# Output projection and the first MLP's first two sets: TensorE's instructions in the order in which they are written

## The chip, the cores and the metric

The kernel runs on one core of a Trainium2 chip. The metric is the device time of one execution in microseconds, the median of the runs. The core has five engines with a queue each: TensorE (PE in the profile, with its weight loads as PEld), VectorE (DVE), ScalarE (ACT), GpSimd (POOL) and SyncE (SP, which here issues most DMAs). Each engine runs its queue in order; an instruction that waits for another engine holds up what stands behind it in its own queue.

## The reference

The model is a two-layer decoder trunk on x of 1024 tokens by 1024 channels, in float32. Layer 0 mixes tokens by a gated linear recurrence with 8 heads, layer 1 by a causal convolution; a squared-ReLU MLP with 4096 hidden units follows each, and every block ends in a DeepNorm layer norm. The change lies where layer 0's mixer ends and its MLP begins:

```python
mix = o.astype(h.dtype) @ w_out                  # o: normalised, gated output of the recurrence
x = layer_norm(DEEPNORM_ALPHA * x + mix, ln_mix_g[0], ln_mix_b[0])
ff = jnp.square(jax.nn.relu(x @ ffn_w1[0])) @ ffn_w2[0]
```

## The kernel before

**Precision and tiles.** Every float32 operand of a large product is split into a high part, rounded to the matrix unit's format, and a low part, the rest. `product` sums high*high, high*low and low*high in one PSUM bank: three matmuls of 128x128 by 128x512 for each 128 of depth. Tokens are split into two halves of 512, a half into four blocks of 128 (t = 0 to 3).

**Seven products in place of eight.** The MLP's products follow Strassen's scheme in the Winograd form: from four quarters of a weight block and four of x come seven forms, taken in the order `ORDER = (1, 2, 6, 5, 7, 3, 4)`. Forms 1 and 2 of x (`xf[1]`, `xf[2]`) come from the first half of the tokens alone, forms 5 and 6 from both halves, forms 7, 3 and 4 last (`x1_late`).

**Output projection** (the loop `for half in range(2)`). A product for token block t and output half n is 8 parts of three matmuls, 24 in all. Three products of the first half, blocks 0, 1, 2 with n = 0, are done earlier, within the tail of the recurrence. The loop then takes for the first half (t, n) = (0,1), (1,1), (3,0), (2,1), (3,1), and for the second all eight in order. DVE adds each result to the residual y. With a block's n = 1 the block is complete, and `x1_block` normalises it: two halves of statistics, their aggregate, an add, a power on POOL, and two scaled passes over the block, all on DVE but the power. It also stores the block (`keep`) and puts jobs on a list, `bg.chores`.

**The list of jobs.** `product` takes one job off the list when its matmuls are written (`bg.chore()`), so a job's instructions stand behind the product that took it. A job of the first half (`turn`) transposes half a block on TensorE (four transposes of 128x128, operands `ident` and `y`) into one of two banks, and ACT and DVE split the result into `xf`. The loop calls `bg.chore()` once more behind `x1_block` of blocks 1, 2 and 3 of the first half. A job of the second half is `x1_first` (four transposes of the left half of the channels, then DVE makes and splits form 5) or `x1_second` (the right half; forms 6, 4 and parts of 3 and 7). For the second half's last block, t = 3, the two are put on the list behind the loop, among empty jobs that only count products.

**The first MLP** (`Up`). Its first matrix is worked through in eight sets c of seven forms; a form is two products (q = 0, 1) of 4 parts, 12 matmuls. Sets 0 and 1 begin out of turn with forms 1 and 2, the early products, from weights split in advance (`early`); then the loop goes on with the forms left, c = 0 and c = 1, and with sets 2 to 7. `fw` loads the four quarters of a set's weights, sums and splits them into forms on DVE and ACT; a buffer of its raw quarters comes free when the last norm of the second half no longer needs its gain and bias.

**Order.** Up to the end of the recurrence all five engines run in the order written (`tc.manual_schedule` with the five engines, closed by `order.close()`). From there on the framework's scheduler chooses each engine's order by its own timing model, and may move an instruction past others that are written earlier, also into the hand-ordered stretch ahead. The names of the profile: `ps` are the eight PSUM banks, `w` and `oT` the projection's operands, `x1f` and `fw` the MLP's, `c` the copies of MLP products, `xf` and `fs` the operands of the layer's input products, whose last ones run in the tail of the recurrence, and `o` the recurrence's output before its own transposes (`ident,o`). Line 204 is the helper through which TensorE and DVE work is recorded.

Of the kernel before, what the change touches and what calls it, by code (L numbers as in the profile page):

```python
# [21 lines left out]
NTB = HT // P  # L22
# [246 lines left out]
def body(ctx, tc, d, out):  # L269
# [10 lines left out]
    def view(kb, shape, dt=F32, name="t"):  # L280
        at, top = int(kb * 1024), KBYTES * 1024
        if at < edge[0]:
            if edge[0] < top:
                space.tile([P, (top - edge[0]) // 4], F32, name="gap")
            edge[0] = 0
        if at > edge[0]:
            space.tile([P, (at - edge[0]) // 4], F32, name="gap")
        edge[0] = at + (prod(shape) + 7) // 8 * 32
        return space.tile([P, *shape], dt, name=name)
# [33 lines left out]
    bg = Background()  # L323
# [47 lines left out]
    order = ExitStack()  # L371
# [12 lines left out]
    def later(n, job):  # L384
        if n:
            waiting.append((ticks[0] + n, job))
        else:
            job()
# [10 lines left out]
    def block_sums(name, layer, c, after=None, gap=0, adds=None):  # L399

        t = sums[name, layer, c] = dram.tile([4, P, 1024], F32, name=f"sum_{name}{layer}{c}")
        v, w = t.rearrange("a p n -> p a n"), d[name][layer, c].rearrange("a p n -> p a n")
        queue = nc.sync if after is not None else nc.gpsimd
        if adds is not None:

            def copies(rows, after):
                nc.sync.dma_start(out=t[0:4:2, rows.start, 0:1], in_=after)
                queue.dma_start(out=v[rows, 0:2], in_=w[rows, 0:4:2])
                queue.dma_start(out=v[rows, 2:4], in_=w[rows, 0:2])

            copies(slice(16, P), after)
            adds.append(lambda after: copies(slice(0, 16), after))
            adds.append(lambda after: nc.gpsimd.dma_start(out=v[:, 0:2], in_=w[:, 2:4], accum_op=ALU.add))
            for i in (2, 3):
                adds.append(lambda after, i=i: nc.gpsimd.dma_start(out=v[:, i], in_=v[:, i - 1], accum_op=ALU.add, max_dma_last_dim=4096))
            return
        if after is not None:
            nc.sync.dma_start(out=t[0:4:2, 0, 0:1], in_=after)
        queue.dma_start(out=v[:, 0:2], in_=w[:, 0:4:2])
        later(gap // 2, lambda: queue.dma_start(out=v[:, 2:4], in_=w[:, 0:2]))  # L420
        parts = [lambda: nc.gpsimd.dma_start(out=v[:, 0:2], in_=w[:, 2:4], accum_op=ALU.add)]
        for i in (2, 3):
            parts.append(lambda i=i: nc.gpsimd.dma_start(out=v[:, i], in_=v[:, i - 1], accum_op=ALU.add, max_dma_last_dim=4096))
        for i, part in enumerate(parts):
            later((i + 1) * gap, part)
# [75 lines left out]
    for k in range(4):  # L501
        c = slice((k % 2) * HT, (k % 2 + 1) * HT)
# [533 lines left out]
    tick(100)  # L1036
    assert not waiting and not loaded and not to_load and not gates, (waiting, gates)
    order.close()
    oT = [o[0] for o in oT]


# [108 lines left out]
    def of(x, t, i=slice(None)):  # L1150
        return x[..., t * P : (t + 1) * P] if i == slice(None) else x[:, i, :, t * P : (t + 1) * P]

    def turned(yt, k0):
        pt = aux()
        for j in range(4):
            tensor.transpose(pt[:, j, :], yt[:, (k0 + j) * P : (k0 + j + 1) * P], ident)
        return pt

    def less(out, x, y):
        vector.tensor_tensor(out=out, in0=x, in1=y, op=ALU.subtract)  # L1160

    def minus_both(out, x, y):
        vector.scalar_tensor_tensor(out=out, in0=x, scalar=-1.0, in1=y, op0=ALU.mult, op1=ALU.subtract)

    def spot(t, k):
        if t < NTB - 1:
            return of(late_x[(7, 3)[k]], NTB - 1)
        return y[1][:, NTB - 2, k * HT : (k + 1) * HT].rearrange("p (a b) -> p a b", a=4)

    def x1_split(i, t, src):  # L1170
        split(of(xf[i], t, 0), of(xf[i], t, 1), src)

    def x1_first(t):
        s, pt = spot(t, 0), turned(y[1][:, t, :], 0)
        less(s, of(xf[1], t, 0).bitcast(F32), pt)
        vector.tensor_tensor(out=s, in0=s, in1=of(xf[1], t, 1).bitcast(F32), op=ALU.add)
        x1_split(5, t, s)
        temp[t], x01[t] = s, pt

    def x1_second(t):  # L1180
        s, pt = spot(t, 1), turned(y[1][:, t, :], 4)
        minus_both(s, temp[t], pt)
        nc.scalar.copy(out=of(late_x[3], t), in_=pt)
        less(of(late_x[7], t), of(late_x[3], t), x01[t])
        x1_split(6, t, s)
        x4 = of(late_x[4], t)
        minus_both(x4, s, of(xf[2], t, 0).bitcast(F32))
        less(x4, x4, of(xf[2], t, 1).bitcast(F32))

    def x1_late(i, k):  # L1190
        nc.gpsimd.tensor_copy(out=xf[i][:, 0, k, :1], in_=fw.queue[0][:, 1, :1].bitcast(F32))
        split(xf[i][:, 0, k : k + 2], xf[i][:, 1, k : k + 2], late_x[i][:, k : k + 2])
# [262 lines left out]
    fw.todo = [[(blocks("w1q", 0, c), 2 if c < 2 else 0)] for c in range(NFC)]  # L1455
    up = Up()

    bg.chores += [lambda: None, lambda: x1_first(NTB - 1), lambda: x1_second(NTB - 1)] + [lambda: None] * 3
    bg.chores += [lambda i=i, k=k: x1_late(i, k) for i in (7, 3, 4) for k in (0, 2)]
    up.form(0, 1, early[0].take(1)[0])  # L1460
    up.form(0, 2, early[1].take(1)[0], late=True)
# [6 lines left out]
    for c in range(NFC):  # L1468
        for i in ORDER[2 if c < 2 else 0 :]:
            (f,) = fw.take(1)  # L1470
            fw.ahead(3)
            if (c, i) == (0, 7):
                bg.done()
            up.form(c, i, f)
        if c in (0, 2):
            block_sums(*to_sum.pop(0), f[:2, 1, :1].bitcast(F32))
        if c == 0:
            up.settle(1)
            hold += [view(208, (2, 1024), F32, "spare"), view(216, (1024,), F32, "next")]
# [478 lines left out]
```

## Time and profile before

| | |
|---|---|
| time, median of 3 runs | 2057.86 us (2054.11 to 2058.38) |
| the profiled execution | 2059.69 us, its span 2057.9 us |
| granted TensorE clock, mean | 0.998 |
| PE busy | 2026.5 us, 98% |
| DVE busy | 1487.4 us, 72% |
| ACT busy | 1092.0 us, 53% |
| POOL busy | 392.1 us, 19% |
| projection's matmuls (w, oT) | x384, 415.7 to 512.5 us |
| first MLP's first product (x1f, fw) | x1344, 513.1 to 827.6 us |

A row of a timeline gives start, length, engine, line, operation, output and inputs, size and count, and in brackets the idle time of the engine ahead of it with the instruction that ended it. Rows of one kind in sequence are merged.

### The profile page before, as it was taken

Reading aid. Unit: us, or ns where it says so; the run is one execution under the profiler, and the core shown is the slowest. Engines: PE = TensorE matmul, PEld = TensorE weight load, DVE = VectorE, ACT = ScalarE, POOL = GpSimd, SP = SyncE. Lnnn points to the kernel's source line nnn. Section 1 sums busy time; section 2 is a strip of 40 time slices with the busy share of each in tenths; the row PEclk is TensorE's granted clock in tenths of the full one; section 3 lists DMA queues with packets and bytes.
Section 4 is the critical chain, followed back from the end, with each engine's and each line's share of the span. In section 5 each row is a group of like instructions: output and inputs, shape, how many; then the busy total and the mean of one; then the engine's idle time right before and its main releaser. Section 6 shows DMA issues by size and latency. Waiting matters only on the chain. (4 is left out here: it accounts for less than half of the span.)

```text
span 2057.9 us, 29631 instructions
## 1 busy us (share of the span) xinstructions
PE 2026.5 (98%) x11144; PEld 1670.6 (81%) x11144; DVE 1487.4 (72%) x1978; ACT 1092.0 (53%) x1725; POOL 392.1 (19%) x393
## 2 busy tenths in 40 slices
PE   8999999999999999999999999999999999999998
PEld 7888887788787888888888888888888887888886
DVE  8698887877966665666567898889589666754456
ACT  5456565631654555444443776488625555443343
POOL 0112222111100000000001699079110000100002
PEclk9999999999999999999999999999999999999999
DMA  4788989842689786999998854587759778995542
GB/s 187 221 200 228 261 240 252 268 187 82 180 295 307 243 286 224 372 338 325 338 336 301 308 185 184 194 330 272 255 215 343 241 231 297 392 294 197 194 154 102
DMA packets 183944, 517.55 MB, mean 251 GB/s; under 512 B 17912, under 2 KB 49784, under 8 KB 182776
## 3 DMA queue, kind: packets, MB, share of 16 engines
q1 hardware_dynamic: 168312, 456.93, 61.8%
q0 software_dynamic: 15488, 58.72, 12.3%
q8 instruction: 87, 1.43, 0.3%
q14 instruction: 57, 0.47, 0.1%
HBM read 380.85 MB, written 201.85 MB: 283 GB/s over the span
## 5 line engine op out<-in xcount | busy, mean ns | idle before, releaser
L204 PE MATMUL ps<-dw,dh 128*128 128x512 f32 x2688 | 611.1, 389 | 0.0
L204 PEld LDWEIGHTS ps<-dw,dh 128*128 128x128 f32 x2688 | 504.2, 188 | 104.6 <-DVE dh L204 0.2
L204 PE MATMUL ps<-x1f,fw 128*128 128x512 f32 x1344 | 309.7, 392 | 4.6 <-ACT c L1266 2.5
L204 PEld LDWEIGHTS ps<-x1f,fw 128*128 128x128 f32 x1344 | 252.5, 189 | 60.3 <-ACT c L1266 3.6
L204 PE MATMUL ps<-xf,fs 128*128 128x512 f32 x1008 | 250.0, 399 | 3.7 <-issue 2.0
L204 POOL TENSOR_TENSOR cb<-cb,prod 128x512 f32<-128x512 f32 x168 | 223.1, 1337 | 12.5 <-ACT prod L1589 2.0
L204 DVE TENSOR_TENSOR dh<-dh 128x1024 fp32r<-128x1024 f32 x112 | 136.5, 1222 | 116.1 <-ACT dh L72 112.7
L204 PEld LDWEIGHTS ps<-xf,fs 128*128 128x128 f32 x1008 | 185.1, 189 | 43.3 <-issue 2.2
L204 DVE SCALAR_TENSOR_TENSOR ps<-u,par,ps 128x512 f32<-128x512 f32 x296 | 206.1, 749 | 11.0 <-ACT ps L1601 9.5
L204 PE MATMUL ps<-xa,wa 128*128 128x512 f32 x864 | 203.0, 392 | 0.1
L72 ACT CAST dh<-dh 128x1024 fp32r<-128x1024 f32 x112 | 117.4, 1051 | 156.0 <-DMA dh<-hf 148.9
L204 PEld LDWEIGHTS ps<-xa,wa 128*128 128x128 f32 x864 | 160.3, 188 | 33.2 <-ACT ha L1331 0.3
L72 ACT CAST dw<-dr 128x1024 fp32r<-128x1024 f32 x112 | 117.3, 1052 | 131.0 <-PE ps L204 115.3
L204 DVE TENSOR_TENSOR dw<-dr,dw 128x1024 fp32r<-128x1024 f32 x112 | 136.3, 1222 | 69.5 <-ACT dw L72 68.4
L1589 ACT ACTIVATE prod<-u,par 128x512 f32<-128x512 f32 x168 | 119.8, 726 | 37.1 <-POOL cb L204 36.7
L518 POOL TENSOR_TENSOR mv<-mv,nhalf 128x1 f32<-128x1 f32 x32 | 42.2, 1321 | 404.8 <-DVE mv L204 394.5
L1450 POOL COPY next<-ss 128x1 f32<-128x1 f32 x38 | 18.9, 497 | 414.5 <-DVE spare L204 255.1
L204 PE MATMUL ps<-w,oT 128*128 128x512 f32 x384 | 89.9, 392 | 1.3 <-ACT oT L932 0.8
L204 PE MATMUL ps<-xb,wa 128*128 128x512 f32 x384 | 91.1, 393 | 0.0
L204 DVE TENSOR_TENSOR spare<-next,spare 128x1024 fp32r<-128x1024 f32 x38 | 46.5, 1224 | 60.4 <-ACT spare L1443 60.3
L204 PE MATMUL ps<-vw,xf 128*128 128x512 f32 x336 | 79.9, 400 | 5.9 <-ACT vw L435 5.3
L204 PEld LDWEIGHTS ps<-w,oT 128*128 128x128 f32 x384 | 71.4, 188 | 16.6 <-ACT oT L932 1.2
(249 smaller groups left out, 2955.9 us busy)
## 6 DMA issues: line engine op xcount, KB each, us to landing
wa<-ready SPq DMA_DIRECT2D x140, 512.0 KB, 4.6
dh<-hf SPq DMA_DIRECT2D x112, 512.0 KB, 5.0
sum_w<-in_w_dram POOLq DMA_DIRECT2D x40, 1024.0 KB, 10.6
ready<-spare SPq DMA_DIRECT2D x76, 512.0 KB, 5.3
raw<-in_w1q_dram SPq DMA_DIRECT2D x66, 512.0 KB, 4.4
dr<-sum_w SPq DMA_DIRECT2D x64, 512.0 KB, 5.7
hf<-ht SPq DMA_DIRECT2D x112, 256.0 KB, 5.1
dr<-in_w_dram SPq DMA_DIRECT2D x48, 512.0 KB, 4.6
```

The lines of the kernel that those rows point to most:

```text
L72: self.nc.scalar.copy(out=slot[:, 0, c], in_=raw[:, c])
L204: return op(*args, **kw)
L518: nc.gpsimd.tensor_tensor(out=dst, in0=src, in1=nhalf[:, :n], op=ALU.pow)
L1450: nc.gpsimd.tensor_copy(out=raw[:, :1], in_=now)
L1589: nc.scalar.activation(tp, u[:, k : k + HT], AF.Copy, scale=tap(j, k))
```

## The change

TensorE, and TensorE alone, is put under an order by hand from the start of the projection to the end of set 1 of the MLP; DVE, ACT, POOL and SP stay with the scheduler. The jobs `x1_first` and `x1_second` of the last block move by one place in the list: there are now two empty jobs ahead of them and two behind them, where there were one and three, so they stand behind the third and the fourth early product instead of the second and the third. The positions of the `x1_late` jobs don't change.

```diff
@@ at the end of the recurrence
     order.close()
+    order.enter_context(tc.manual_schedule(engines={mybir.EngineType.PE}))
     oT = [o[0] for o in oT]
@@ ahead of the early products
-    bg.chores += [lambda: None, lambda: x1_first(NTB - 1), lambda: x1_second(NTB - 1)] + [lambda: None] * 3
+    bg.chores += [lambda: None] * 2 + [lambda: x1_first(NTB - 1), lambda: x1_second(NTB - 1)] + [lambda: None] * 2
     bg.chores += [lambda i=i, k=k: x1_late(i, k) for i in (7, 3, 4) for k in (0, 2)]
@@ in the loop over the MLP's sets
         if c in (0, 2):
             block_sums(*to_sum.pop(0), f[:2, 1, :1].bitcast(F32))
+        if c == 1:
+            order.close()
```

## The prediction

> **What bounds the kernel now.** I read the page's busy times first, then the table of stretches around the edit, then TensorE's waits there.
>
> ```profile
> PE 2026.5 (98%) x11144; PEld 1670.6 (81%) x11144; DVE 1487.4 (72%) x1978; ACT 1092.0 (53%) x1725; POOL 392.1 (19%) x393
> ...
> 415.70:513.00 97.30, 96.78 (x455) 80.25 (x456) 74.60 (x106) 25.41 (x42) 10.82 (x8) 1.00 0.34 128
> 513.00:536.60 23.60, 23.58 (x112) 19.24 (x110) 20.59 (x29) 11.51 (x17) 1.45 (x1) 1.00 0.40 131
> 536.60:552.00 15.40, 13.47 (x50) 10.30 (x50) 14.24 (x14) 11.05 (x14) 6.71 (x7) 0.89 0.83 269
> ...
> PE ps L204 <- ACT c L1266: 2.5, 4, 1.3
> PE ps L204 <- ACT fw L72: 1.5, 1, 1.5
> PE ps L204 <- ACT oT L932: 0.8, 1, 0.8
> ```
>
> Columns of a stretch: length, then busy time (instructions) of PE, weight load, DVE, ACT, POOL, then the granted clock, DMA share and GB/s. The output projection ends at 513.0, the first MLP starts there. TensorE is busy 96.78 of 97.30 us in the projection, so a microsecond of waiting added there is a microsecond of kernel time. Nearly all that the edit can win lies in the third stretch: 1.93 us idle and a clock of 0.89. The waits are us in total, times, longest, from 412 to 830 us: 2.5 us for ACT's copies (c), mostly in later sets, 1.5 for the MLP's weights (fw), 0.8 for the projection's input (oT).
>
> Next I read TensorE in order of time, because the edit is an edit of that order.
>
> ```profile
> 413.28 1.62 PE L204 MATMUL ps<-xf,fs 128*128 128x512 f32 x6
> 415.70 0.73 PE L204 MATMUL ps<-w,oT 128*128 128x512 f32 x2 [0.80 <-ACT oT L932]
> 416.96 1.20 PE L204 MATMUL ps<-w,oT 128*128 128x512 f32 x4 [0.52 <-DVE oT L204]
> 417.99 0.60 PE L204 MATMUL ps<-ident,o 128*128 128x128 f32 x4
> ...
> 419.82 1.53 PE L204 MATMUL ps<-w,oT 128*128 128x512 f32 x6
> 421.18 0.60 PE L204 MATMUL ps<-ident,o 128*128 128x128 f32 x4
> 421.54 1.64 PE L204 MATMUL ps<-xf,fs 128*128 128x512 f32 x6
> 423.01 33.06 PE L204 MATMUL ps<-w,oT 128*128 128x512 f32 x145
> 455.91 1.03 PE L204 MATMUL ps<-ident,y 128*128 128x128 f32 x8
> 456.70 6.39 PE L204 MATMUL ps<-w,oT 128*128 128x512 f32 x27
> 462.92 1.03 PE L204 MATMUL ps<-ident,y 128*128 128x128 f32 x8
> 463.71 5.70 PE L204 MATMUL ps<-w,oT 128*128 128x512 f32 x24
> 469.26 1.03 PE L204 MATMUL ps<-ident,y 128*128 128x128 f32 x8
> ```
>
> A matmul takes (33.06 - 0.39) / 144 = 0.227 us from start to start, 0.39 being one matmul's own length on this page's larger groups, so a projection product of 24 takes 5.44 us and an MLP product of 12 takes 2.72. Eight transposes move the next matmul by 456.70 - 455.91 = 0.79 us, four by 0.40.
>
> Two things are to be seen. First, matmuls of the projection stand between the transposes of the recurrence (ident,o) although all of them are written behind it: the scheduler filled holes of the tail with the third written product, block 3's left half. Secondly, the transposes of y come late. The first pair of groups comes after 2+4+6+145 = 157 matmuls, where the code has it after 120 (three early products, then two). The third pair comes after 208, where the code has the first of it, block 2's left half, after 168: directly behind the product that finishes block 2. The scheduler put them off because y wasn't normalised. The written order doesn't.
>
> **The change part by part.** It adds and removes no instruction and no transfer. It fixes TensorE's order from the projection to the end of set 1, and shifts two of TensorE's groups with the three plus five DVE and two plus two ACT operations that hang on them; no DMA, nothing on POOL or SP. What is queued behind a waiting transpose is every later matmul.
>
> Part 1, **two transposes in front of an unfinished normalisation.** In the first half's loop, `product` takes one job off the list, `x1_block` normalises, and then `bg.chore()` takes another. By the counts of the list, the job taken there is behind product (1,1) an old block's second half, but behind (2,1) it is block 2's own left half and behind (3,1) block 3's own. These must wait for this chain:
>
> ```profile
> 459.49 0.69 DVE L204 SCALAR_TENSOR_TENSOR y<-y,ps 128x512 f32<-128x512 f32 x1
> 460.21 0.69 DVE L204 BATCH_NORM_STATS2 bs<-y 128x6 f32<-128x512 f32 x1
> 460.94 0.21 DVE L204 BATCH_NORM_AGGREGATE mv<-bs 128x2 f32<-128x12 f32 x1
> 461.18 0.15 DVE L204 TENSOR_SCALAR mv<-mv 128x1 f32<-128x1 f32 x1
> 461.25 1.27 DVE L204 SCALAR_TENSOR_TENSOR y<-y,mv,ln_mix_g 128x1024 f32<-128x1024 f32 x1
> 462.96 1.28 DVE L204 SCALAR_TENSOR_TENSOR y<-y,mv,ln_mix_b 128x1024 f32<-128x1024 f32 x1 [0.44 <-POOL mv L518]
> 464.18 1.29 DVE L204 TENSOR_TENSOR x1f<-ps,x1f 128x512 fp32r<-128x512 f32 x2
> ```
>
> That is (2,1): from 459.49 to 462.96 + 1.28 = 464.24, 4.75 us from the product's end to a finished y. Now it is hidden by the next product, 16 of whose matmuls run before the next transposes. In the written order only the four transposes of the product's own job (0.40) stand in between: a wait of about 4.4 us, allowing little for the signal, and the same behind (3,1). Bounds: 4.2 each, if DVE starts at once; 5.0, if half of the last row quoted (0.65, the split of the old block's transposes) gets in first. I take 4.4, since 4.75 was measured with the chain alone on DVE: 8.8 for both. The other written places have cover: block 0 and 1 have a whole product (5.44) behind their normalisation.
>
> Part 2, **the clock after a wait.**
>
> ```profile
> 347.45 1.08 PE L204 MATMUL ps<-xf,fs 128*128 128x512 f32 x4 [2.02 <-issue]
> 539.04 12.78 PE L204 MATMUL ps<-x1f,fw 128*128 128x512 f32 x48 [1.48 <-ACT fw L72]
> 659.21 36.08 PE L204 MATMUL ps<-x1f,fw 128*128 128x512 f32 x156 [1.25 <-ACT c L1266]
> ...
> 348.80:352.20 3.40, 3.32 (x9) 2.48 (x8) 1.71 (x4) 2.99 (x9) 1.06 (x2) 0.50 1.06 252
> 539.95:543.35 3.40, 3.40 (x10) 2.55 (x9) 3.40 (x4) 0.65 (x2) 2.50 (x1) 0.50 0.66 233
> 659.40:662.80 3.40, 3.40 (x16) 2.74 (x16) 3.37 (x4) 1.68 (x3) 0.77 (x1) 1.00 0.92 324
> ```
>
> Idle times of 2.02 and 1.48 us are each followed by 3.4 us at a clock of 0.50; one of 1.25 us isn't. Half speed for 3.4 us loses 1.7. Per 4.4 us wait I bound this by 1.2 (1.0 us of the slow stretch falls into the wait itself) and 2.3 (0.6 in a slow stretch half used up by the wait, then a whole one), and take 1.7: 3.4 for both.
>
> Part 3, **the tail's holes come back.** The written order puts block 3's left half behind (1,1), so the 6 matmuls at 415.70 and the 6 at 419.82 leave the holes they filled; the 9 that lie within the 145 only change places.
>
> ```profile
> 416.05 1.16 ACT L741 ACTIVATE o<-ps,ss 128x128 f32<-128x128 f32 x4
> 418.52 1.20 ACT L741 ACTIVATE o<-ps,ss 128x128 f32<-128x128 f32 x4
> ```
>
> The recurrence's transposes then start when these end, near 417.3 and 419.85 instead of 417.99 and 421.18. That gains 1.33, against 12 x 0.227 = 2.72 of work still to be done: a loss of 1.4. The hole from 414.90 to 417.3 is longer than both idle times that halved the clock, and 1.83 us of matmuls stand behind it, of which the wait for the second group hides 0.7: up to 1.0 more. I take 2.2, ends 1.4 and 2.4. [...]
>
> Part 4, **the second half's blocks.** Their first group is written one product after the normalisation's, 5.44 + 0.40 behind the end of the product. For blocks 1 and 2 the five DVE operations of the block before (about 0.6 each, half of a 1.28 pair) compete with the chain: 4.75 + 3.0 = 7.75, a wait of up to 1.9 each; lower bound 0. I take 0.3 each, 0.6, since DVE is busy 74.60 of 97.30 us there and the new waits leave it less behind.
>
> Part 5, **what is won at the MLP's start.**
>
> ```profile
> 527.34 0.60 PE L204 MATMUL ps<-ident,y 128*128 128x128 f32 x4
> ...
> 528.01 0.60 PE L204 MATMUL ps<-ident,y 128*128 128x128 f32 x4
> ...
> 528.65 0.69 DVE L204 TENSOR_TENSOR y<-x1f,ps 128x512 f32<-128x512 f32 x1 [2.24 <-PE ps L204]
> ...
> 533.76 1.22 DVE L204 TENSOR_TENSOR sum<-raw 128x1024 f32<-128x1024 f32 x1
> ...
> 539.50 2.35 DVE L204 TENSOR_TENSOR fw<-sum,fw 128x1024 fp32r<-128x1024 f32 x2
> ```
>
> Block 3's transposes stand 14.3 us into the MLP (527.34), DVE waits for them, its eight operations run to 533.8, and only then come the weight sums, which TensorE awaits at 539.04 for 1.48 us. Written behind the third product they come 3 x 2.72 = 8.2 us in, when the chain of 4.75 has ended; DVE is free 6 us earlier against the same need. So the third stretch's 1.93 idle and the slow stretch's 1.7 can go: at most 3.6, at least 0 if another operand is next. Next late are the pieces of the late forms (x1f of form 7), needed four products or 10.9 us behind those weights. I take 3.0.
>
> Part 6, products no longer interleave, so a bank's copy has two products (5.44 us) to be done. No row shows such a wait unfilled; bounds 0 and 2.5 (all waits for copies together), taken 0.3, near 0, since 513.0 to 536.6 has the same copies and is idle for 0.02 us.
>
> **Sum**: 8.8 + 3.4 + 2.2 + 0.6 - 3.0 + 0.3 = 12.3 us. The profiled execution took 2059.7 (span 2057.9), 1.8 above the median of 2057.86; so 2072.0 under the profiler and 2070.2 in the median. All ends together: 8.4 + 2.4 + 1.4 + 0 - 3.6 + 0 = +8.6; and 10.0 + 4.6 + 2.4 + 3.8 - 0 + 2.5 = +23.3.
>
> **The rivals.**
>
> *TensorE passes the waiting transposes* (the other side; the change doesn't do what it says). Place: behind (2,1) and (3,1). If the order by hand binds only loosely, the next product goes ahead of block 2's and block 3's halves, and parts 1 and 2 vanish; with the holes still filled, part 5 alone remains, whole: -3.6, 2054.3. It decides from the first of these groups that stands behind matmuls of the next product. For it: the holes of a hand-written stretch were filled by outsiders. Against: within it those written keep their order, and here nothing is left outside.
>
> *The waits are paid back.* If the MLP's sets are paced by weights, copies and sums, these run ahead while TensorE waits. The whole of part 5 goes, and the 2.5 us of later waits for copies: 8.8 + 3.4 + 2.2 - 3.6 - 2.5 = +8.3, 2066.2. For it: DVE 20.59 of 23.60 us at the MLP's start. Against: TensorE is busy for 98%, and weight slots bound the lead.
>
> *The second half waits as well.* Part 4 at its upper end, 3.8, each wait over 1.48 and so slowing the clock, 3.4: 12.3 - 0.6 + 7.2 = +18.9, 2076.8. For it: DVE's five competing operations come first in the code. Against: in a wait of TensorE nothing new arrives for DVE, so it catches up.
>
> *Only one of the two waits is real*, the other hidden: 6.1 less, and part 3 at 1.4, part 5 whole: 12.3 - 6.1 - 0.8 - 0.6 = +4.8 at most, and with parts 4 and 6 gone +3.9: 2061.8, within what can be told.
>
> **How the numbers follow.** Forecast 0.56, paid back 0.15, second half 0.17, only one wait 0.05, passing 0.07. The time is the forecast's, 2070. 0.2% of the time, 4.1 us, is about what a measurement of this kernel can tell from no change: faster 0.07 (passing), within 0.05 (one wait), slower 0.88. The range takes in "paid back" with a margin of 3 and reaches to "second half": 2063 to 2077, narrower than the ends added up since these won't all fall on one side.
>
> **What would show it.** In the changed trace: transposes of y after 120, 144, 168 and 192 projection matmuls; ahead of those after 168 and 192, TensorE idle 4 to 5 us for DVE's y, with a clock of 0.50 in the 3 us behind each; no projection matmul ahead of 421 us and idle TensorE from 415 to 417; no wait for fw at the MLP's start. I am wrong if those two idle times are under 2 us each, or if the MLP's sets 0 and 1 lose more than they did.

## The result: 2083.9 us, 1.3% slower

The changed kernel takes 2083.91 us in the median (2078.86 to 2092.44, 6 runs), beside 2058.05 us before (2054.11 to 2061.58, 6 runs): ratio 1.013, 95% interval 1.0106 to 1.0153. The sign and the first cause were as predicted; the size was 26 us instead of 12, and the time lies outside the range.

The profiled execution has a span of 2080.0 us. First TensorE's waits from 412 to 860 us (us in total, times, longest), then its timeline:

```profile
PE ps L204 <- DVE y L204: 15.1, 5, 4.9
PE ps L204 <- ACT o L741: 2.8, 2, 2.4
PE ps L204 <- ACT c L1267: 2.1, 1, 2.1
PE ps L204 <- ACT fw L72: 2.1, 1, 2.1
PE ps L204 <- DVE fw L204: 1.5, 1, 1.5
PE ps L204 <- DVE t L204: 0.5, 1, 0.5
```

```profile
410.12 1.62 PE L204 MATMUL ps<-xf,fs 128*128 128x512 f32 x6
414.10 0.66 PE L204 MATMUL ps<-ident,o 128*128 128x128 f32 x4 [2.36 <-ACT o L741]
...
420.50 26.14 PE L204 MATMUL ps<-w,oT 128*128 128x512 f32 x114 [0.47 <-DVE t L204]
446.48 1.03 PE L204 MATMUL ps<-ident,y 128*128 128x128 f32 x8
...
458.75 0.60 PE L204 MATMUL ps<-ident,y 128*128 128x128 f32 x4
464.23 1.12 PE L204 MATMUL ps<-ident,y 128*128 128x128 f32 x4 [4.88 <-DVE y L204]
464.99 6.78 PE L204 MATMUL ps<-w,oT 128*128 128x512 f32 x24
471.62 0.60 PE L204 MATMUL ps<-ident,y 128*128 128x128 f32 x4
477.09 0.76 PE L204 MATMUL ps<-ident,y 128*128 128x128 f32 x4 [4.88 <-DVE y L204]
477.50 7.34 PE L204 MATMUL ps<-w,oT 128*128 128x512 f32 x24
...
496.42 5.72 PE L204 MATMUL ps<-w,oT 128*128 128x512 f32 x24
...
510.04 0.66 PE L204 MATMUL ps<-ident,y 128*128 128x128 f32 x4 [1.98 <-DVE y L204]
...
524.10 0.66 PE L204 MATMUL ps<-ident,y 128*128 128x128 f32 x4 [1.98 <-DVE y L204]
524.51 7.36 PE L204 MATMUL ps<-w,oT 128*128 128x512 f32 x24
531.71 0.60 PE L204 MATMUL ps<-ident,y 128*128 128x128 f32 x4
532.06 8.46 PE L204 MATMUL ps<-x1f,fw 128*128 128x512 f32 x36
541.88 0.66 PE L204 MATMUL ps<-ident,y 128*128 128x128 f32 x4 [1.37 <-DVE y L204]
...
558.73 0.73 PE L204 MATMUL ps<-x1f,fw 128*128 128x512 f32 x2 [2.08 <-ACT fw L72]
560.92 99.34 PE L204 MATMUL ps<-x1f,fw 128*128 128x512 f32 x426 [1.46 <-DVE fw L204]
```

No projection matmul stands in the recurrence's tail any more, and TensorE is idle there for 2.36 us. The transposes of y stand where they are written, after 120, 144, 168 and 192 projection matmuls, with 4.88 us of waiting behind each of the two products named in the prediction. Not forecast, or not at this size, are the waits for blocks 1 and 2 of the second half (1.98 each, forecast as 0.3) and for block 3 (1.37), and the waits for weights at the MLP's start, 2.08 and 1.46, where 1.48 stood before. The clock, in its four slow stretches up to 600 us (columns as in the prediction; a fifth, of 3.4 us, stands behind the wait for copies at 682 us):

```profile
463.85:467.27 3.42, 3.04 (x9) 2.57 (x10) 1.01 (x2) 0.59 (x1) 0.00 (x0) 0.50 0.38 153
477.50:480.92 3.42, 3.42 (x11) 2.75 (x10) 1.37 (x2) 0.59 (x1) 0.00 (x0) 0.50 0.38 153
525.30:528.70 3.40, 3.40 (x9) 2.66 (x8) 2.56 (x4) 0.70 (x2) 0.00 (x0) 0.50 0.27 106
559.43:566.25 6.82, 5.36 (x14) 4.17 (x14) 5.98 (x6) 2.43 (x4) 4.64 (x2) 0.50 0.87 307
```

**Where the time went.** The two executions aren't at the same time when the edit begins: the last matmuls ahead of the tail start at 410.12 instead of 413.28, a difference within the recurrence, whose own instructions the edit doesn't touch (in the traces of the experiments this matmul starts at 411.3 to 415.8 us). From there to the MLP's first matmul it is 532.06 - 410.12 = 121.94 us, before 513.13 - 413.28 = 99.85 with four transposes (0.40) still to come: the projection lost 21.7. The MLP's first product lasts, from its first to its last matmul, by the group of these matmuls

```profile
L204 PE MATMUL ps<-x1f,fw x1344: 387/389/796, 532.1 to 849.8; 128*128 128x512 f32 x192
```

317.7 us, before 827.6 - 513.1 = 314.5 with the 0.4 in it: 3.6 lost. From its last matmul to the end of the span it is 1230.2 us, before 1230.3. Then 21.7 + 3.6 - 3.2 = 22.1, the difference of the spans. So the loss lies in the stretch under the edit, and nothing is given back behind it.

| | predicted | measured |
|---|---|---|
| tail of the recurrence (part 3) | +2.2 | +2.1 |
| two waits for an unfinished block (part 1) | +8.8 | +9.8 |
| slow clock behind these (part 2) | +3.4 | +3.0 |
| second half: waits and slow clock (part 4) | +0.6 | +5.6 |
| rest of the projection (not traced further) | | +1.2 |
| first MLP (parts 5 and 6) | -2.7 | +3.6 |
| sum | +12.3 | +25.3 |

The tail: from 410.12 to 446.48, 36.4 us; before, from 413.28 to 455.91 less the 37 matmuls done more, 34.2. The slow clock: 24 matmuls took 6.78, 7.34 and 7.36 us instead of 5.72, and the four transposes ahead of the first 24 moved the next matmul by 464.99 - 464.23 = 0.76 us instead of 0.40. The second half: 1.98 twice, and 7.36 - 5.72 = 1.6 of slow clock. Two terms of the six hold 11 of the 13 us that were missed.

### The profile page after: what moved, and what is told of

Same layout as the page of the kernel before. It is cut to its first block, busy times and chain, and to the rows that moved or that the text cites. A ratio compares the mean times of both kernels' runs of the same rounds, so it can differ in the third digit from the quotient of the medians.

```text
span 2080.0 us, 29627 instructions
## 1 busy us (share of the span) xinstructions
PE 2030.9 (98%) x11144; PEld 1674.7 (81%) x11144; DVE 1488.1 (72%) x1978; ACT 1093.1 (53%) x1725; POOL 394.4 (19%) x393
## 5 line engine op out<-in xcount | busy, mean ns | idle before, releaser
L1592 ACT ACTIVATE prod<-u,par 128x512 f32<-128x512 f32 x168 | 119.7, 726 | 36.4 <-POOL cb L204 35.6
L204 PE MATMUL ps<-w,oT 128*128 128x512 f32 x384 | 94.7, 406 | 0.5 <-DVE t L204 0.5
```

Source lines behind the costliest of these rows:

```text
L204: return op(*args, **kw)
L1592: nc.scalar.activation(tp, u[:, k : k + HT], AF.Copy, scale=tap(j, k))
```

## Experiments

All ratios are to the kernel before, run beside each kernel; its medians there were 2061.3 to 2063.3 us, so the absolute times in the expectations, which were made from 2058, are some 4 us low. Only ratios and differences are compared.

### The two edits apart

The order alone, with the old list of jobs:

```diff
-    bg.chores += [lambda: None] * 2 + [lambda: x1_first(NTB - 1), lambda: x1_second(NTB - 1)] + [lambda: None] * 2
+    bg.chores += [lambda: None, lambda: x1_first(NTB - 1), lambda: x1_second(NTB - 1)] + [lambda: None] * 3
```

> The order by hand alone, with the old list of jobs (block 3's transposes behind the second and third early product). Theory: the loss belongs to the order, and the shift only softens it. Block 3 was finished 10.0 us behind its product; two early products and four transposes cover 5.8 of it, three cover 8.6, so the wait of 1.4 us for block 3 becomes about 4 and the time is 2 to 4 us over the changed kernel's 2083.9. Rival: the shift of the jobs costs something of its own; then this kernel is several us below 2083.9.

Measured: ratio 1.0137 (1.0117 to 1.0158). TensorE's waits for y are 18.0 us instead of 15.1, 2.9 more, as expected; in the time the two kernels can't be told apart.

The shift alone is the kernel before with the other line of the same diff:

> The shift of the two jobs alone, TensorE's order left to the scheduler. Theory: the scheduler places these transposes by its own readiness (it had them 14.3 us into the MLP), so their written place hardly matters: within 4 us of 2058. Rival: the written place decides when block 3's forms and the weights are made; then the MLP's start changes by up to the 3.6 us it loses, 2054, or by as much the other way.

Measured: ratio 1.0005 (0.999 to 1.002). In its trace TensorE waits for fw for 1.5 us at 538 us, as before. The loss belongs to the order; without it the shift makes no difference that can be told.

### The transposes directly behind their own product

```diff
                 x1_block(half, t)
-                if half == 0 and t:
-                    bg.chore()
```

> The changed kernel without the second bg.chore() behind the first half's blocks, so that no block's transposes stand directly behind its own product. Theory (the losses add up): the two waits of 4.88 us and the two slow stretches of 3.4 us behind them go, 9.8 + 3.4 = 13.2 us: 2071. Rival (what TensorE waits there the other engines use, and give back later): under 6 us of it is seen, above 2078.

Measured: ratio 1.0051 (1.0034 to 1.0068), some 16 us under the changed kernel's 1.013; with both intervals that is 10 to 22, and 13.2 was expected. TensorE's wait for y falls from 15.1 to 5.4 us:

```profile
PE ps L204 <- DVE y L204: 5.4, 3, 2.0
```

The two waits of 4.88 are gone with their slow stretches, and what is left are the three shorter ones. A wait of 1.2 us for `x1f` has come in the first half. The losses add up: this is the largest one.

### The second half's jobs one product later

On top of the last kernel:

```diff
             bg.done()
+            bg.chores.append(lambda: None)
...
-    bg.chores += [lambda: None] * 2 + [lambda: x1_first(NTB - 1), lambda: x1_second(NTB - 1)] + [lambda: None] * 2
+    bg.chores += [lambda: None] * 2 + [lambda: x1_first(NTB - 1), lambda: x1_second(NTB - 1)] + [lambda: None]
```

> The kernel without the extra job, and with the second half's jobs one product later: an empty job ahead of them, one fewer behind, so that two products instead of one stand between a block's last product and its first transposes, and block 3's come behind the fourth early product. Theory: the waits of 1.98 us for blocks 1 and 2, the slow stretch behind one of them (1.7) and the wait of 1.4 for block 3 go, 7 us under the kernel without the extra job, which was 9.4 over before: about 2.4 over before, with no wait of TensorE for y. Rival: DVE has as much to do either way, so the waits turn up at the next operand that DVE makes; then under 2 us are won.

Measured: ratio 1.001 (0.9999 to 1.0021; the medians are 4.1 us apart), by the ratios some 8 us under the kernel without this edit. No wait for y is left. The term of the second half is confirmed, together with block 3's wait: one product isn't cover enough for a block's normalisation in the second half, two are.

### The weights at the MLP's start

The first form split in the loop (form 6 of set 0) went into the buffer at 144 KB, which the last early product still reads. The five buffers, named here by their place in KB, are used in turn, as a ring; the ring is turned, on the changed kernel:

```diff
-    fw = Forms(nc, vector, slots((144, 152, 48, 112, 120), "fw"), ...
+    fw = Forms(nc, vector, slots((152, 48, 144, 112, 120), "fw"), ...
```

> The changed kernel with the ring of the MLP's weight buffers turned, so that the first split form no longer goes into the buffer that the last early product still reads. Theory: that buffer sets the wait at the MLP's start (the split's high part began 1.0 us behind the end of the last product that reads the buffer); then the waits of 2.08 and 1.46 us and the slow stretch of 6.8 us behind them go, 6.9 us in all: 2077. Rival (my prediction's own chain: the raw weights come late because their buffers hold block 3's gain and bias until it is normalised): no change over 1 us, 2083 to 2085.

Measured: ratio 1.0118 (1.01 to 1.0137), not clear of the changed kernel's. The trace decides. TensorE's timeline of this kernel:

```profile
549.25 52.10 PE L204 MATMUL ps<-x1f,fw 128*128 128x512 f32 x228
603.11 75.45 PE L204 MATMUL ps<-x1f,fw 128*128 128x512 f32 x324 [1.77 <-ACT c L1267]
683.01 17.17 PE L204 MATMUL ps<-x1f,fw 128*128 128x512 f32 x68 [4.46 <-ACT c L1267]
```

From the fifth early product on it runs for 52 us without a wait: both waits for weights are gone, so the shared buffer made them. But TensorE then waits 1.77 and 4.46 us for copies (c), where the changed kernel waited 2.1. The win is largely spent there.

Does the written order help the MLP, taken alone? Here the order by hand starts at the first early product, in the second run with the ring turned as well; the third is the kernel before with the ring turned and nothing else.

> The order by hand from the first early product on alone; the projection stays with the scheduler. Theory: TensorE loses at the MLP's start by its fixed order, since it can't take up form 5 while form 6's weights wait for their buffer; the changed kernel lost 3.6 us more there than before, so 2 to 4 over before. Rival (my prediction's part 5): 3 under before.

> The same with the weight buffers turned, so that form 6's weights are split into a buffer that is free. Theory: no wait for weights at the MLP's start is left, which removes all of the 3.6 us that the kernel before loses there: 2 to 4 under before, unless the later waits for copies grow as they did with the turned buffers under the changed kernel (4.5 us in set 3), then within 2 of before. Rival: the written order waits elsewhere in sets 0 and 1; then over before.

> The kernel before with the weight buffers turned and nothing else. Theory: the shared buffer is also what the kernel before waits for at 539 us; the wait of 1.48 us and the slow stretch of 1.7 go, about 3 under before. Rival: the scheduler keeps the same order of its forms and TensorE waits for block 3's forms or the weights' sums instead; within 1 us of before.

Measured: 1.0015 (1.0004 to 1.0026), 1.0007 (0.9995 to 1.002) and 0.999 (0.9979 to 1.0). So the written order in the MLP alone costs some 3 us (0.8 to 5.4) even with an undisturbed projection, where I had predicted a gain of 3. In the second run the waits for weights are gone but for 0.4 us, and the win isn't seen in the time: the theory's exception came, 6.0 us for a copy at 667 us (5.3 in the first run). In both runs block 3's transposes wait 2.7 us, with y ready: for the PSUM bank that block 2's job, left late by the scheduler's projection, still reads. In the third the wait for fw stays, 1.4 us: the scheduler's own order doesn't hang on that buffer.

### The waits for copies near 660 us

ACT's timeline of the changed kernel at its wait of 2.1 us for a copy (TensorE goes on at 682.4):

```profile
679.83 1.05 ACT L1444 CAST spare<-next 128x1024 fp32r<-128x1024 f32 x1 [3.74 <-DMA next<-in_wpw_dram]
680.78 1.04 ACT L72 CAST fw<-raw 128x1024 fp32r<-128x1024 f32 x1
681.73 1.06 ACT L1267 COPY c<-ps 128x512 f32<-128x512 f32 x2
```

The copies stand in ACT's queue behind the split of a weight of a later layer, loaded ahead (`spare`), which waits for its DMA. I took the sums of the second matrix's blocks, made by DMA and started in set 2, for what makes that DMA late, and put them off to set 4, in two kernels beside a third for comparison:

```diff
-        if c in (0, 2):
+        if c in (0, 4):
             block_sums(*to_sum.pop(0), f[:2, 1, :1].bitcast(F32))
```

> The kernel with the later jobs, and with the weight buffers turned. Theory (what the MLP's start wins is given back in set 2 or 3, where ACT stands behind a weight preload that the busy DMA brings late): the waits for weights of 1.1 and 1.5 us go, the wait for copies near 660 us, 3.6 before, grows by about as much; the time stays within 2 of the kernel with the later jobs alone (4.1 over before). Rival (the waits simply add up): 2.6 or more under it, about 1.5 over before.

> The same, and the second block of weight sums, which DMA makes during set 2, put off to set 4. Theory: these sums (2 MB copied and three accumulations) make the DMA late near 660 us; without them ACT's preloads land earlier, the wait for copies there falls from about 4 to 6 us to under 2, and the win at the MLP's start is seen: 1 over to 2 under before. Rival: the stores of the hidden values or the preloads alone fill the DMA; the wait stays over 3 us, or moves to set 4.

> The kernel before with that block of sums put off to set 4 and nothing else, as the control. Theory: its wait of 1.25 us at 659 us goes, 1 to 2 under before. Rival: no change, within 1.

Measured: 0.9995 (0.9983 to 1.0008) without the sums' shift; with it 1.0039 (1.0023 to 1.0054), and 1.0024 (1.0014 to 1.0034) for the kernel before with the sums put off. Waits of TensorE in the second of these:

```profile
PE ps L204 <- ACT c L1266: 8.6, 1, 8.6
PE ps L204 <- DVE fw L204: 2.8, 1, 2.8
```

There is no wait near 660 us in either kernel with the sums put off; instead one of 8.6 us at 736 and one of 7.1 us at 733 us, in the later set. The wait follows the sums, so they cause it (that they do it through late loads is read from ACT's rows, not tested apart), but the place in set 2 is the better one, and the rival (the wait moves) was right. In the first kernel the two waits for weights became one of 2.8 us, for the low part; and the wait for copies didn't grow, against my theory: it fell from 4.3 to 1.7 us, and the kernel is by the ratios 3 us under the one with the old ring, though the intervals overlap. With the three edits together, no extra job, later jobs and the turned ring, the whole loss of the written order is gone: 0.9995 of the kernel before. How large that wait is in a given kernel stays unexplained: it was 1.25 to 6 us in the kernels here with the sums in set 2.

### The best written order

The order by hand from the second half of the projection on, with the later jobs and the turned ring; first with the sums in set 4, then back in set 2; then with block 3's transposes behind the third early product again.

```diff
     for half in range(2):
+        if half == 1:
+            order.enter_context(tc.manual_schedule(engines={mybir.EngineType.PE}))
```

> The order by hand from the second half of the projection on only (the first half and with it the filling of the recurrence's holes stays with the scheduler), later jobs, turned buffers, sums put off. Theory: all four losses that the written order brought are gone (2.1 in the recurrence's tail, the first half's and the second half's waits, the MLP's weights), and the 3.6 us that the kernel before lost at the MLP's start too: 3 to 5 under before. Rival: the scheduler puts block 3's transposes of the first half so late that the written order waits at its beginning, or the later waits for copies take the win back: within 1.5 of before.

> The order by hand from the second half of the projection on, later jobs, turned buffers, the weight sums back in set 2. Theory (the losses add up): the tail's 2.1 us less than the same with the whole projection by hand, which was within 1 of before; so 1 to 4 under before. Rival (the later wait for copies takes it): within 1 of before.

> The same with block 3's transposes behind the third early product instead of the fourth. Theory (DVE's amount of work sets when the first form is split): the wait of 2.8 us for its low part stays within 0.7, and a wait of TensorE for y of 1 to 2 us is added: 1 to 2 over the other run. Rival (the transposes' place sets it): the wait shrinks by up to 2.7, the time of a product, and the time is under the other run's.

Measured: 1.002 (1.0009 to 1.0031), 0.9986 (0.9976 to 0.9996) and 1.0008 (0.9996 to 1.0019). The first has the wait of the later set again, 6.6 us. The second is the only kernel here that is clear of the kernel before and under it: 2058.36 us beside 2063.34. With fourteen kernels compared, one that lies so little beyond its interval can be chance. It is 1.9 us under the one with the whole projection by hand, the later jobs and the turned ring (0.9995), as the tail's 2.1 us ask; the intervals overlap, and this kernel also keeps the extra job of the first half, whose place the scheduler chooses.

The pair differs in one place of one job. TensorE at the MLP's start, the kernel with the fourth product:

```profile
527.95 8.97 PE L204 MATMUL ps<-x1f,fw 128*128 128x512 f32 x38
539.70 20.47 PE L204 MATMUL ps<-x1f,fw 128*128 128x512 f32 x89 [2.79 <-DVE fw L204]
```

and the one with the third:

```profile
523.58 0.66 PE L204 MATMUL ps<-ident,y 128*128 128x128 f32 x4 [1.12 <-DVE xl L204]
...
527.17 33.14 PE L204 MATMUL ps<-x1f,fw 128*128 128x512 f32 x143
```

The wait for weights is gone and 1.12 us of waiting ahead of the transposes has come (for the bank that block 2's job reads, y being ready): the place of block 3's transposes does set when the first form is split, as the prediction's part 5 had it and against my theory here. But the copies are then waited for longer, 7.5 us with 5.4 the longest, against 3.2, and the time is higher, by the ratios some 4.5 us. Whether this is the same win given back or chance of the scheduler's order on ACT, the runs don't tell.

## Why the prediction was wrong

Two terms of the sum failed: part 4, the second half's waits, mis-sized (0.6, measured 5.6), and part 5, the gain at the MLP's start (3.0), which came out as a loss (3.6).

**Part 1 was right**, a little low. The second of the two chains on DVE:

```profile
471.81 0.69 DVE L204 SCALAR_TENSOR_TENSOR y<-y,ps 128x512 f32<-128x512 f32 x1 [5.13 <-PE ps L204]
472.54 0.69 DVE L204 BATCH_NORM_STATS2 bs<-y 128x6 f32<-128x512 f32 x1
473.15 0.67 DVE L204 TENSOR_TENSOR x1f<-ps,x1f 128x512 fp32r<-128x512 f32 x1
...
475.75 1.28 DVE L204 SCALAR_TENSOR_TENSOR y<-y,mv,ln_mix_b 128x1024 f32<-128x1024 f32 x1 [0.44 <-POOL mv L518]
```

From 471.81 to 477.03, 5.2 us, with one split of the old block's transposes in it: the case that I had as the upper end, 5.0, and not the 4.4 taken. **Part 2** was right for these two (3.0 for 3.4), but not its rule, that an idle time as long as 1.48 us slows the clock (see the last section). **Part 3** was right in the sum, 2.1 for 2.2, by luck: the hole of 2.36 us didn't slow the clock. Instead TensorE waited 0.47 us for a DVE instruction that writes `t` soon behind it, which with the 1.4 of the lost matmuls makes 1.9.

**Part 4 failed by its size.** I bounded each wait by 1.9 us and took 0.3, arguing that DVE catches up while TensorE waits. Both came to 1.98, the upper end, and the second brought a slow stretch that I had left out of the term. DVE for block 1 of the second half:

```profile
502.17 0.69 DVE L204 SCALAR_TENSOR_TENSOR y<-y,ps 128x512 f32<-128x512 f32 x1 [2.05 <-PE ps L204]
502.77 0.68 DVE L204 SCALAR_TENSOR_TENSOR xl<-xl,ps 128x512 f32<-128x512 f32 x1
...
508.10 0.69 DVE L204 SCALAR_TENSOR_TENSOR y<-y,ps 128x512 f32<-128x512 f32 x1 [0.32 <-PE ps L204]
508.70 1.28 DVE L204 SCALAR_TENSOR_TENSOR y<-y,mv,ln_mix_b 128x1024 f32<-128x1024 f32 x1
```

The chain takes 502.17 to 509.98 = 7.8 us, my worst case of 7.75. Being ahead is of no use to DVE here: it was idle for 2.05 us when the chain began. The five competing operations belong to a job whose transposes stand directly behind the same product, so both become ready at the same moment, in every block, however far DVE has caught up. The next product's result was taken in ahead of the last pass as well (508.10).

**Part 5 failed by its sign.** Three things were against the step "DVE is free 6 us earlier against the same need". First, block 3's own normalisation was not over in 4.75 us: from 531.91 to 541.83 it took 9.9 (6.0 in the kernel before, 512.98 to 518.95). Besides the five operations of block 2's job, DVE's queue had splits of the early weights in it, one of which waited for ACT and its load:

```profile
534.30 0.20 DVE L204 BATCH_NORM_AGGREGATE mv<-bs 128x2 f32<-128x12 f32 x1
535.22 1.23 DVE L204 TENSOR_TENSOR fw<-raw,fw 128x1024 fp32r<-128x1024 f32 x1 [0.71 <-ACT fw L72]
...
540.55 1.28 DVE L204 SCALAR_TENSOR_TENSOR y<-y,mv,ln_mix_b 128x1024 f32<-128x1024 f32 x1
```

Hence the wait of 1.37 behind the third early product. Second, the split for the next weights (form 6) waited for its buffer, not for the sums. ACT and DVE of the changed kernel, then ACT of the run with the ring turned:

```profile
557.65 1.03 ACT L72 CAST fw<-sum 128x1024 fp32r<-128x1024 f32 x1
...
559.65 1.22 DVE L204 TENSOR_TENSOR fw<-sum,fw 128x1024 fp32r<-128x1024 f32 x1
```

```profile
556.66 1.05 ACT L72 CAST fw<-sum 128x1024 fp32r<-128x1024 f32 x1
```

The sum was ready at 551.7; the high part was begun at 557.65, about 1 us after the last early product had read the buffer (556.66), and the low part 2 us later. TensorE waits for either. The row alone doesn't name the buffer, since the scheduler put other splits ahead of it on ACT; the turned ring does: there the high part begins at 556.66, some 3.5 us before the last early product ends (549.25 + 48 x 0.227 = 560.1), and both waits vanish. Third, with the buffer free and the jobs later, DVE itself is full. The kernel with the whole projection by hand, later jobs and the turned ring, from 520 to 551 us:

```profile
520.00:551.00 31.00, 28.21 (x125) 22.83 (x126) 29.84 (x39) 16.32 (x23) 5.60 (x4) 0.94 0.51 175
```

DVE is busy 29.84 of 31.00 us and TensorE still waits 2.8 for its low part. The same row of before (20.59 of 23.60) stood in the prediction, as an argument for a rival; it should have been a bound on this term. And I followed the wait of before back to the sum, but didn't ask what would bind next:

```profile
537.94 1.04 ACT L72 CAST fw<-sum 128x1024 fp32r<-128x1024 f32 x1 [0.56 <-DVE sum L204]
```

The split of before did wait for the sum, and turning the ring there changes nothing. But by the count of its matmuls (four forms of 24, taken as the first 96) the last early product had read the buffer only at 528.37 + 8.21 = 536.58, 1.4 us ahead: by this estimate an earlier sum could win that much at most, whatever DVE's lead. It is the lower end that the prediction named, "at least 0 if another operand is next", and didn't take.

**Part 6**, waits for copies in sets 0 and 1, was 0 there, in place of 0.3.

**The rivals.** The second half's waits were the best of them in kind and size (+18.9); with part 5 at nothing instead of its gain it comes to +21.9. TensorE did not pass the waiting transposes. Both waits of part 1 were real. Nothing was paid back. The sign of being wrong that the prediction named last came true: the MLP's sets 0 and 1 lost more than they did.

## What to carry to other kernels

Before an order is fixed by hand, go through the list of jobs and count, for each, what work stands between the last result that it needs and its own place: a job that the scheduler quietly put off by a product becomes a wait of the whole chain. Cost that chain as it is in the loop's steady state, with the operations that become ready at the same moment put ahead of it, not as it was measured alone. And when a wait is to be won, look past what ends it now to what would end it next: here a buffer that another product was still reading.

## What the runs showed of the hardware

TensorE's clock fell to 0.50 in stretches. In the changed kernel's clock records they start at 463.86, 477.51, 525.30, 559.43 and 682.31 us and last 3.41 us, the fourth 6.83; in those of the kernel before they start at 348.79 and 539.93 us and last 3.41 (from 11 us to each kernel's last matmul). Beside them the idle times of TensorE over 1.1 us in the same stretch of the two traces, in us:

| idle for | in | slow stretch starts |
|---|---|---|
| 4.88 | after | 0.4 ahead of its end |
| 4.88 | after | 0.4 behind its end |
| 2.36 | after | none |
| 2.15 | after | at its end |
| 2.08, then 1.46 | after | 0.7 behind the end of the first, 6.83 long |
| 2.02 | before | 1.3 behind its end |
| 1.98 | after | none |
| 1.98 | after | 1.2 behind its end |
| 1.87 | after | none |
| 1.48 | before | 0.9 behind its end |
| 1.37 | after | none |
| 1.25 | before | none |
| 1.20 | after | none |

So the length of an idle time alone doesn't tell in these two traces whether the clock falls: of the two waits of 1.98 us the first kept it and the second lost 7.36 - 5.72 = 1.6 us in the 24 matmuls behind it, and the idle time of 2.36 us kept it where one of 1.48 didn't. What else decides was not shown.
